# Memory of x given early to half of the left forms, in a hybrid RWKV-7 and short-convolution block

## The chip, the core and the metric

The kernel runs on one core of a Trainium2 chip. Five engines matter here: TensorE (PE in the profile) multiplies 128x128 weights with up to 512 columns; VectorE (DVE), ScalarE (ACT) and GpSimd (POOL) work on rows of 128 partitions; SyncE (SP) issues most transfers. Each engine works through its own queue in order, and the engines wait for one another by semaphores. The metric is the time of one execution in microseconds (us).

## The reference: what is computed

The input x has 512 rows of 2048 numbers; 16 learned meta rows are put ahead, which makes 528. Cut to what matters here:

```python
hn = _rmsnorm(h_res, norm_in_g[l])
P = hn @ w_in[l]                      # 528 x 2048 times 2048 x 8320
Pr, Pc = P[..., :RW_COLS], P[..., RW_COLS:]
...                                   # group A: RWKV-7 recurrence on r, k, v, decay, a; gate g_r
y_a = (yn + bonus) * jax.nn.silu(g_r)
Bg, Cg, hc, g_c = (four parts of Pc, 1024 columns each)
y_b = Bg * _causal_depthwise_conv(Cg * hc, conv_w[l]) * jax.nn.silu(g_c)
mix = jnp.concatenate([y_a, y_b], axis=-1)
h_res = h_res + mix @ w_out[l]        # 512 x 2048 times 2048 x 2048
out = _rmsnorm(h_res, norm_f_g)
```

All of it is float32. The change concerns the end of the first product (`w_in`) and the beginning of the last one (`w_out`).

## The kernel before, in words

**Split numbers.** TensorE multiplies in a shorter format (float32r). To keep float32's accuracy, each operand is split into a high part, which ACT makes by a cast, and a low part, which DVE makes by subtracting the high part from the original. A product is three matmuls: high by high, high by low, low by high. For x the parts are `xh` and `xl`, two tiles of 16 column blocks (k) by 528 rows, filled by `split_x` at the start. For a half piece of weights they are `wh` and `wl` (`split_w`, L124 and L125) in the projection, `oh` and `ol` (`split_unit`, L1171 and L1172) in the output projection. The buffers of these pieces rotate: six of each.

**The projection.** `main` runs one tile of 128 output columns at a time, in 65 tiles. A tile goes through k in four quarters (`k4`), and `steps` issues the matmuls of one quarter (L312). After a tile, `use` evacuates PSUM with the row scale (`scaled`, L331) and does the tile's own arithmetic. The last four tiles are C, h, B and gc of convolution block 7; for gc the arithmetic is L331 on DVE, tanh on ACT (L358), and on DVE L359 and L422, which writes block 15 of the mix. L359 reads scratch tiles of the pool `tp`.

**The mix and the left forms.** `mix` is four tiles of four column blocks by 512 rows: tiles 0 and 1 are the recurrence's blocks 0 to 7, tiles 2 and 3 the convolution's blocks 8 to 15. `split_mix` finishes a block and splits it (L1061, L1062; tile `m`). The output projection is done by a Strassen-like scheme with seven products, M1, P5, M7, M3, Q6, P4 and M2. Four of them take sums of quarters of the mix on the left: `sums(q)` (L1070 to L1075) forms these sums in place, for half q of the column blocks, by four DVE operations on 128x1024 numbers; `split_form(f, q)` (L1117, L1118; tile `S`) splits one of the four forms S1, S3, S4, S5 of half q by one ACT cast and one DVE subtraction of 128x1024. Each form occupies two tiles of 128x1024 numbers in the pool `pw`.

**Order of the output projection.** `units` is a list of (half, product, group): first the four groups of M1, then for each group P5, M7, M3 and Q6, then P4 and M2; and the same for the second half. A unit is 12 matmuls of 512 columns with one group of rows of w_out, in two pieces. Groups 0 and 1 use the forms of half q = 0, groups 2 and 3 those of q = 1. In the profile's names the product's letter is shown without its digit, so that M1, M7, M3 and M2 are all `M`; M1 reads `m` on the left, the others of the first four groups `S`. `at(u, fn, ...)` puts work ahead of unit u: in the kernel before, `split_form(f, 0)` is called at units 0 to 3, `sums(1)` at unit 3 and `split_form(f, 1)` at units 6 to 9. The right-hand pieces for M1's groups 0 to 2 are loaded and split during the projection (the stream's last three entries). Group 3's rows go into a tile of `pw` (`begin_chain`, L1148), a pool that takes the place of the projection's pools when these are closed (`ph1.close()`, L1100).

**What sets the order.** PE's order is written by hand: the generator `flow` yields matmul by matmul, and `fill`, `step` and the loops interleave other work. For DVE, ACT, POOL and SP the planner of the tile framework sets the order, by the position in the program, by `tc.high_priority` (the weight splits have it) and by when it reckons an operand to be ready; `tc.issue_after(ins)` puts an instruction behind `ins` on the same engine. A tile that takes over memory waits for the last reader of the tile that had it (`reuse_waits="tile"`).

Of the kernel before, what the change touches and what calls it, by code (L numbers as in the profile page):

```python
# [9 lines left out]
F32 = mybir.dt.float32  # L10
# [8 lines left out]
P = 128  # L19
DM = 2048  # L20
KT = DM // P
# [55 lines left out]
def hymba_kernel(ctx: ExitStack, tc: tile.TileContext, xt, xtok, front, w_in, w_out, pv, lup, cst, msk, gf, out):  # L77
# [62 lines left out]
    cq = ph2.enter_context(tc.tile_pool(name="cq", bufs=1, side="right", reuse_waits="tile"))  # L140
    ph1 = ExitStack()
    xp = ph1.enter_context(tc.tile_pool(name="xp", bufs=1))
    xh = xp.tile([P, KT, L], F32R, name="xh")
    xl = xp.tile([P, KT, L], F32R, name="xl")
    rs = xp.tile([P, L], F32, name="rs")
    la = xp.tile([P, 2, L], F32R, name="la")
    ones = xp.tile([P, P + 2], F32R, name="ones")
# [8 lines left out]
    scr_x = [dp.tile([SCR], F32, tag=f"sx{b}", name=f"sx{b}", bufs=1) for b in range(2)]  # L156

    tp = ph1.enter_context(tc.tile_pool(name="tp", bufs=1))

    def tr(name, dt=F32):  # L160
        return cq.tile([P, LP], dt, tag="tr", name=name, bufs=5)
# [28 lines left out]

    def split_x(kt, cols=slice(0, L)):
        gain = ng[:, kt : kt + 1]
        nc.scalar.activation(xh[:, kt, cols], raw[kt][:, cols], AF.Copy, scale=gain)
        return nc.vector.scalar_tensor_tensor(
            out=xl[:, kt, cols], in0=raw[kt][:, cols], scalar=gain, in1=xh[:, kt, cols].bitcast(F32),
            op0=ALU.mult, op1=ALU.subtract,
        ).ins

# [104 lines left out]
    def steps(ps, ranges, k4, q, ks=range(4), rs_=range(2)):  # L303
        hi, lo = quarters[q]
        for r, (a, b) in enumerate(ranges):
            if r not in rs_:
                continue
            for k in ks:
                kt = 4 * k4 + k
                w = slice(k * P, (k + 1) * P)  # L310
                for n, (ww, xx) in enumerate(((hi, xh), (hi, xl), (lo, xh))):
                    nc.tensor.matmul(  # L312
                        ps[r], ww[:, w], xx[:, kt, a:b], start=(kt == 0 and n == 0), stop=(kt == KT - 1 and n == 2)
                    )
                    yield (b - a) * 0.43

# [747 lines left out]

    forms = {"S3": (0, T1), "S5": (0, T0), "S1": (2, T1), "S4": (2, T0)}

    def quarter(k, tk, q):
        return mix[2 * k + q][:, :, tk]

    def sums(q):  # L1070
        a11, a21, a12, a22 = quarter(0, T0, q), quarter(0, T1, q), quarter(1, T0, q), quarter(1, T1, q)
        nc.vector.tensor_tensor(out=a22, in0=a22, in1=a21, op=ALU.subtract)
# [40 lines left out]
    def split_form(f, q):  # L1113
        k, tk = forms[f]
        x = mix[k + q][:, :, tk]
        hi, lo = sform[f, q]
        nc.scalar.copy(hi, x)  # L1117
        nc.vector.tensor_tensor(out=lo, in0=x, in1=hi.bitcast(F32), op=ALU.subtract)  # L1118


    LEFT = {"M1": 0, "M2": T0, "M7": "S3", "Q6": "S5", "P5": "S1", "P4": T1, "M3": "S4"}
# [41 lines left out]
    def split_unit(unit, t, home=None):  # L1163
        for q in range(2):
            rq = t()[:, q * 512 : (q + 1) * 512]
            if home is None:
                hi = wp.tile([P, 512], F32R, tag="hi", name=f"oh{U[unit]}{q}", bufs=6)
                lo = wp.tile([P, 512], F32R, tag="lo", name=f"ol{U[unit]}{q}", bufs=6)
            else:
                hi, lo = home[q]  # L1170
            nc.scalar.copy(hi, rq)  # L1171
            nc.vector.tensor_tensor(out=lo, in0=rq, in1=hi.bitcast(F32), op=ALU.subtract)  # L1172
            right[unit, q] = (hi, lo)

    def here(t, n):
# [148 lines left out]
    for u, unit in enumerate(units):  # L1324
# [150 lines left out]
```

## Time and profile before

| what | value |
|---|---|
| median of 3 timed runs | 1026.73 us (1024.77 to 1630.5) |
| profiled execution | 1021.34 us |
| its span (first to last instruction) | 1019.6 us |
| PE busy | 1005.0 us, 99% of the span |
| DVE busy | 684.2 us, 67% |
| ACT busy | 394.6 us, 39% |
| POOL busy | 274.7 us, 27% |
| last projection tile (gc of block 7) on PE | 840.27 us, for 11.14 us |
| output projection on PE, first unit | 851.24 us |

The profile is that of one execution; all times within it count from the start of the span. The profiled execution's own time is that of the span and what lies around it, and the timed runs are others. PE is busy almost throughout, so that what counts is where it is not: the waits of PE, what ends them, and the chain of work that ended last. "Busy" for PE is modelled, because matmuls overlap; the start of one matmul against the start of the next shows lost time more truly than the idle column.

### The profile page before, as it was taken

Reading aid. Unit: us, or ns where it says so; the run is one execution under the profiler, and the core shown is the slowest. Engines: PE = TensorE matmul, PEld = TensorE weight load, DVE = VectorE, ACT = ScalarE, POOL = GpSimd, SP = SyncE. Lnnn points to the kernel's source line nnn. Section 1 sums busy time; section 2 is a strip of 40 time slices with the busy share of each in tenths; the row PEclk is TensorE's granted clock in tenths of the full one; section 3 lists DMA queues with packets and bytes.
Section 4 is the critical chain, followed back from the end, with each engine's and each line's share of the span. In section 5 each row is a group of like instructions: output and inputs, shape, how many; then the busy total and the mean of one; then the engine's idle time right before and its main releaser. Section 6 shows DMA issues by size and latency. Waiting matters only on the chain.

```text
span 1019.6 us, 23707 instructions
## 1 busy us (share of the span) xinstructions
PE 1005.0 (99%) x9723; PEld 917.8 (90%) x9723; DVE 684.2 (67%) x1235; ACT 394.6 (39%) x727; POOL 274.7 (27%) x294
## 2 busy tenths in 40 slices
PE   9999999999999999999999999999999999999996
PEld 7899998999998999998999998889889897787885
DVE  7877765568655569654669653244555697999786
ACT  7544322534322434322424322222222335445453
POOL 0132323323232323232323222223332332005001
PEclk9999999999999999999999999999999999999999
DMA  9436386364864263853273846877672687695644
GB/s 315 146 106 167 84 219 189 98 166 103 214 171 138 84 168 102 216 150 117 83 178 100 209 139 180 299 225 235 194 229 86 197 272 189 168 320 138 173 124 165
DMA packets 184892, 174.82 MB, mean 171 GB/s; under 512 B 121552, under 2 KB 142672, under 8 KB 184400
## 3 DMA queue, kind: packets, MB, share of 16 engines
q1 hardware_dynamic: 182192, 164.40, 54.1%
q0 software_dynamic: 2304, 8.39, 4.8%
q8 instruction: 76, 1.25, 0.5%
q10 hardware_dynamic: 288, 0.52, 0.1%
q14 instruction: 32, 0.26, 0.1%
HBM read 136.92 MB, written 36.35 MB: 170 GB/s over the span
## 4 chain that ended last, share of the span: by engine, by line
PE 90%; DVE 4%; DMA 3%; ACT 1%; issue 1%; SPq 0%; DVEq 0%; POOL 0%; ACTq 0%
PE ps_v L312 9%; PE ps_h L312 9%; PE ps_g L312 9%; PE ps_B L312 9%; PE ps_gc L312 9%; PE ps_k L312 9%; PE ps_C L312 8%; PE ps_r L312 8%; PE M L1199 4%; PE P L1199 3%; PE Q L1199 2%; PE g L638 2%; DVE ol L1172 1%; PE zs L963 1%; PE zy L967 1%
## 5 line engine op out<-in xcount | busy, mean ns | idle before, releaser
L125 POOL TENSOR_TENSOR wl<-wr,wh 128x512 fp32r<-128x512 f32 x121 | 170.3, 1408 | 371.6 <-ACT wh L124 349.4
L124 ACT CAST wh<-wr 128x512 fp32r<-128x512 f32 x254 | 154.0, 618 | 299.1 <-PE ps_k L312 52.3
L125 DVE TENSOR_TENSOR wl<-wr,wh 128x512 fp32r<-128x512 f32 x133 | 98.9, 752 | 107.3 <-ACT wh L124 106.2
L312 PE MATMUL ps_v<-xh,wh 128*128 128x264 f32 x256 | 73.1, 286 | 0.0
L312 PE MATMUL ps_k<-xh,wh 128*128 128x264 f32 x256 | 73.0, 285 | 0.0
L312 PE MATMUL ps_h<-xh,wh 128*128 128x258 f32 (+1 forms) x256 | 72.9, 285 | 0.1
L312 PE MATMUL ps_k<-xh,wl 128*128 128x264 f32 x256 | 73.0, 285 | 0.0
L312 PE MATMUL ps_r<-xh,wl 128*128 128x258 f32 (+1 forms) x256 | 72.1, 282 | 0.7 <-DVE wl L125 0.7
L312 PE MATMUL ps_v<-xh,wl 128*128 128x264 f32 x256 | 72.7, 284 | 0.0
L312 PE MATMUL ps_v<-xl,wh 128*128 128x264 f32 x256 | 72.7, 284 | 0.0
L312 PE MATMUL ps_k<-xl,wh 128*128 128x264 f32 x256 | 72.6, 284 | 0.0
L312 PE MATMUL ps_C<-xh,wh 128*128 128x258 f32 (+1 forms) x256 | 72.6, 284 | 0.0
L312 PE MATMUL ps_g<-xl,wh 128*128 128x258 f32 (+1 forms) x256 | 72.4, 283 | 0.0
L312 PE MATMUL ps_h<-xh,wl 128*128 128x258 f32 (+1 forms) x256 | 72.2, 282 | 0.0
L312 PE MATMUL ps_r<-xh,wh 128*128 128x258 f32 (+1 forms) x256 | 72.1, 282 | 0.0
L312 PE MATMUL ps_C<-xl,wh 128*128 128x258 f32 (+1 forms) x256 | 72.0, 281 | 0.0
L312 PE MATMUL ps_r<-xl,wh 128*128 128x258 f32 (+1 forms) x256 | 72.0, 281 | 0.0
L312 PE MATMUL ps_g<-xh,wh 128*128 128x258 f32 (+1 forms) x256 | 72.0, 281 | 0.0
L312 PE MATMUL ps_h<-xl,wh 128*128 128x258 f32 (+1 forms) x256 | 71.9, 281 | 0.0
L312 PE MATMUL ps_g<-xh,wl 128*128 128x258 f32 (+1 forms) x256 | 71.9, 281 | 0.0
L312 PE MATMUL ps_C<-xh,wl 128*128 128x258 f32 (+1 forms) x256 | 71.9, 281 | 0.0
L312 PE MATMUL ps_B<-xl,wh 128*128 128x512 f32 x128 | 51.0, 399 | 0.0
(344 smaller groups left out, 3001.2 us busy)
## 6 DMA issues: line engine op xcount, KB each, us to landing
wr<-in_w_in_dram SPq DMA_DIRECT2D x127, 512.0 KB
ct<-opd SPq DMA_DIRECT2D x64, 288.0 KB
wo<-in_w_out_dram SPq DMA_DIRECT2D x24, 512.0 KB
x<-in_w_out_dram POOLq DMA_DIRECT2D x16, 512.0 KB, 5.6
opd<-ar SPq DMA_DIRECT2D x8, 576.0 KB
opd<-gt SPq DMA_DIRECT2D x16, 288.0 KB
opd<-bt SPq DMA_DIRECT2D x64, 64.0 KB
x<-in_w_out_dram SPq DMA_DIRECT2D x8, 512.0 KB
```

The source lines that it names most:

```text
L124: nc.scalar.copy(hi, rq)
L125: low[q] = eng.tensor_tensor(out=lo, in0=rq, in1=hi.bitcast(F32), op=ALU.subtract).ins
L312: nc.tensor.matmul(ps[r], ww[:, w], xx[:, kt, a:b], start=(kt == 0 and n == 0), stop=(kt == KT - 1 and n == 2))
L638: nc.tensor.matmul(z[h][:, c - c0], bk[hs, c, h : h + 2, :].rearrange("p a s -> p (a s)"), ar[hs, c].rearrange("p a s -> p (a s)"), start= ...
L963: nc.tensor.matmul(d[hs, j], w, x[hs], start=(a == 0), stop=(a == b - 1))
L967: nc.tensor.matmul(d[ho, j], t[hs, o : o + CH], x[hs], start=(a == 0), stop=(a == b - 1))
L1172: nc.vector.tensor_tensor(out=lo, in0=rq, in1=hi.bitcast(F32), op=ALU.subtract)
L1199: nc.tensor.matmul(bank[s], left(prod, jj, m, s), w, start=(jj == 0 and n == 0), stop=(jj == 7 and n == 2))
```

## The change

The two tiles `xh` and `xl` become eight, one for each quarter of k. The first two quarters of both lie in a pool `xq` of their own, the other two in `xp`. When the last projection tile has issued its first two quarters (`k4 == 2`), `xq` is closed, and a pool `ps` with the forms of half q = 0 is opened; those four forms are split there at once, ahead in the program of the rest of that tile and its evacuation. `sums(1)` is done in two parts: column blocks 0 to 2 of the half (of 128x768 numbers) before the last projection tile's `step` loop, block 3 (128x256) at unit 3, as before. The forms of q = 1 are called at units 6 to 9 as before, but by `late_form`, which puts them behind the last split that the program issued by unit 1. The home tiles of the second half's M2 pieces, which reuse the forms' memory, come from `ps` too.

```diff
-    xh = xp.tile([P, KT, L], F32R, name="xh")
-    xl = xp.tile([P, KT, L], F32R, name="xl")
...
+    ph0 = ExitStack()
+    xq = ph0.enter_context(tc.tile_pool(name="xq", bufs=1))
+    xh, xl = ([(xq if k4 < 2 else xp).tile([P, 4, L], F32R, name=f"{n}{k4}") for k4 in range(4)] for n in ("xh", "xl"))
...
-        nc.scalar.activation(xh[:, kt, cols], raw[kt][:, cols], AF.Copy, scale=gain)
+        hi, lo = (x[kt // 4][:, kt % 4, cols] for x in (xh, xl))
+        nc.scalar.activation(hi, raw[kt][:, cols], AF.Copy, scale=gain)
...
-                        ps[r], ww[:, w], xx[:, kt, a:b], start=(kt == 0 and n == 0), stop=(kt == KT - 1 and n == 2)
+                        ps[r], ww[:, w], xx[k4][:, k, a:b], start=(kt == 0 and n == 0), stop=(kt == KT - 1 and n == 2)
...
+            if k4 == 2 and j == len(plan) - 1:
+                state["half"] = True
...
-    def sums(q):
-        a11, a21, a12, a22 = quarter(0, T0, q), quarter(0, T1, q), quarter(1, T0, q), quarter(1, T1, q)
+    def sums(q, rows=slice(0, 4)):
+        a11, a21, a12, a22 = (mix[2 * k + q][:, rows, tk] for k in range(2) for tk in (T0, T1))
...
+    sform = {}
+
+    def new_forms(pool, q):
+        for f in forms:
+            sform[f, q] = [pool.tile([P, 4, HT], F32R, tag=f"{f}{q}{a}", name=f"{f}{q}{a}") for a in range(2)]
...
     for j in range(NPAIR + 4, KT):
+        if j == KT - 1:
+            sums(1, slice(0, 3))
+            while "half" not in state:
+                step()
+            ph0.close()
+            ps = ctx.enter_context(tc.tile_pool(name="ps", bufs=1, side="right", reuse_waits="tile"))
+            new_forms(ps, 0)
+            for f in ("S1", "S3", "S4", "S5"):
+                split_form(f, 0)
         while ("gc", j - NPAIR) not in ready:
             step()
...
-    sform = {
-        (f, q): [pw.tile([P, 4, HT], F32R, tag=f"{f}{q}{a}", name=f"{f}{q}{a}") for a in range(2)]
-        for q in range(2) for f in forms
-    }
+    new_forms(pw, 1)
...
+    def late_form(f):
+        with tc.issue_after(state["first"]):
+            split_form(f, 1)
...
-            nc.vector.tensor_tensor(out=lo, in0=rq, in1=hi.bitcast(F32), op=ALU.subtract)
+            state["last"] = nc.vector.tensor_tensor(out=lo, in0=rq, in1=hi.bitcast(F32), op=ALU.subtract).ins
...
-            pw.tile([P, 4, HT], F32R, tag=f"{f}0{a}", name=f"home{g}{a}").rearrange("p a b -> p (a b)") for a in range(2)
+            ps.tile([P, 4, HT], F32R, tag=f"{f}0{a}", name=f"home{g}{a}").rearrange("p a b -> p (a b)") for a in range(2)
...
     for n, f in enumerate(("S1", "S3", "S4", "S5")):
-        at(n, split_form, f, 0)
         if n == 2:
-            at(n + 1, sums, 1)
-        at(6 + n, split_form, f, 1)
+            at(n + 1, sums, 1, slice(3, 4))
+        at(6 + n, late_form, f)
...
+        if u == 1:
+            state["first"] = state["last"]
```

More of the change, by code (lines that the diff above doesn't have):

```diff
@@ L192, in split_x @@
         gain = ng[:, kt : kt + 1]
-        nc.scalar.activation(xh[:, kt, cols], raw[kt][:, cols], AF.Copy, scale=gain)
+        hi, lo = (x[kt // 4][:, kt % 4, cols] for x in (xh, xl))
+        nc.scalar.activation(hi, raw[kt][:, cols], AF.Copy, scale=gain)
         return nc.vector.scalar_tensor_tensor(
-            out=xl[:, kt, cols], in0=raw[kt][:, cols], scalar=gain, in1=xh[:, kt, cols].bitcast(F32),
+            out=lo, in0=raw[kt][:, cols], scalar=gain, in1=hi.bitcast(F32),
             op0=ALU.mult, op1=ALU.subtract,
@@ L1065, in hymba_kernel @@
     forms = {"S3": (0, T1), "S5": (0, T0), "S1": (2, T1), "S4": (2, T0)}
-    def quarter(k, tk, q):
-        return mix[2 * k + q][:, :, tk]
-    def sums(q):
-        a11, a21, a12, a22 = quarter(0, T0, q), quarter(0, T1, q), quarter(1, T0, q), quarter(1, T1, q)
+    def sums(q, rows=slice(0, 4)):
+        a11, a21, a12, a22 = (mix[2 * k + q][:, rows, tk] for k in range(2) for tk in (T0, T1))
         nc.vector.tensor_tensor(out=a22, in0=a22, in1=a21, op=ALU.subtract)
@@ L1091, in hymba_kernel, with split_form @@
     chain.update({g: new_chain(0, g) for g in range(3)})
-    for j in range(NPAIR + 4, KT):
+    sform = {}
+    def new_forms(pool, q):
+        for f in forms:
+            sform[f, q] = [pool.tile([P, 4, HT], F32R, tag=f"{f}{q}{a}", name=f"{f}{q}{a}") for a in range(2)]
+    def split_form(f, q):
+        k, tk = forms[f]
+        x = mix[k + q][:, :, tk]
+        hi, lo = sform[f, q]
+        nc.scalar.copy(hi, x)
+        nc.vector.tensor_tensor(out=lo, in0=x, in1=hi.bitcast(F32), op=ALU.subtract)
+    for j in range(NPAIR + 4, KT):
+        if j == KT - 1:
[7 more added lines that the diff above has]
+                split_form(f, 0)
         while ("gc", j - NPAIR) not in ready:
@@ L1106, in hymba_kernel @@
     fv = pw.tile([P, 4, 3], F32, name="fv")
-    sform = {
-        (f, q): [pw.tile([P, 4, HT], F32R, tag=f"{f}{q}{a}", name=f"{f}{q}{a}") for a in range(2)]
-        for q in range(2) for f in forms
-    }
+    new_forms(pw, 1)
     xa = [pw.tile([P, 1024], F32, name=f"xa{t}") for t in range(4)]
[L1113 to L1118, printed above, removed]
+    def late_form(f):
+        with tc.issue_after(state["first"]):
+            split_form(f, 1)
     LEFT = {"M1": 0, "M2": T0, "M7": "S3", "Q6": "S5", "P5": "S1", "P4": T1, "M3": "S4"}
```

## The prediction

> **What bounds the kernel now.** I first read how busy each engine is and which engines make up the chain that ended last.
>
> ```profile
> span 1019.6 us, 23707 instructions
> PE 1005.0 (99%) x9723; PEld 917.8 (90%) x9723; DVE 684.2 (67%) x1235; ACT 394.6 (39%) x727; POOL 274.7 (27%) x294
> PE 90%; DVE 4%; DMA 3%; ACT 1%; issue 1%; SPq 0%; DVEq 0%; POOL 0%; ACTq 0%
> ```
>
> PE is idle for 1019.6 - 1005.0 = 14.6 us in all, and the chain runs over PE for nine tenths of the span. The change neither adds nor removes a matmul. So whatever it gives must come out of those 14.6 us, which are 1.4% of the span. A gain of 2% is not there to be had. Next come PE's waits by releaser, and in the timeline of PE the places in the reach of the change.
>
> ```profile
> PE M L1199 <- DVE ol L1172: 1.0, 3, 0.5
> PE Q L1199 <- DVE ol L1172: 0.6, 1, 0.6
> ...
> 851.24 0.40 PE L1199 MATMUL M<-wh,m 128*128 128x512 f32 x1
> ...
> 860.40 0.50 PE L1199 MATMUL M<-ol,m 128*128 128x512 f32 x1 [0.22 <-DVE ol L1172]
> ...
> 863.07 0.40 PE L1199 MATMUL P<-oh,S 128*128 128x512 f32 x1
> ...
> 870.30 0.50 PE L1199 MATMUL M<-ol,S 128*128 128x512 f32 x1 [0.53 <-DVE ol L1172]
> ...
> 873.23 0.50 PE L1199 MATMUL Q<-ol,S 128*128 128x512 f32 x1 [0.56 <-DVE ol L1172]
> ...
> 875.90 0.39 PE L1199 MATMUL P<-oh,S 128*128 128x512 f32 x1
> ...
> 939.12 0.50 PE L1199 MATMUL M<-ol,m 128*128 128x512 f32 x1 [0.27 <-DVE ol L1172]
> ...
> 890.29 5.60 PE M L1199 x24
> ```
>
> All four waits of the output projection are for `ol`, the low part of a piece of w_out, which DVE writes at L1172. The modelled idle times add up to 1.6 us, but the starts tell more. The last row is an undisturbed run of 24 matmuls in 5.60 us, or 2.80 us for a unit of 12. From 851.24 the four M1 units should end at 862.44, but the first P5 unit starts at 863.07: **0.63 us lost in the fourth M1 unit**. From there four units should end at 874.27, but the next starts at 875.90: **1.63 us lost in M3 and Q6 of group 0**. The wait at 939.12 is worth 0.27 us.
>
> What makes DVE late there is shown by the chain in order of time, and by the busy time of each engine in three stretches (PE, PEld, DVE, ACT, POOL in that order).
>
> ```profile
> 851.44 0.70 DVE gc L331
> ...
> 852.83 0.70 DVE gc L359
> ...
> 853.55 5.36 DMA x<-in_w_out_dram
> ...
> 859.00 0.63 ACT oh L1171
> ...
> 859.66 0.56 DVE ol L1172
> ...
> 872.57 0.61 DVE ol L1172
> ...
> 838.50:851.40 12.90, 12.90 (x57) 10.49 (x56) 7.33 (x11) 4.00 (x8) 6.08 (x4) 1.00 0.82 201
> 851.40:862.90 11.50, 11.28 (x48) 8.65 (x48) 10.11 (x13) 8.48 (x13) 1.76 (x2) 1.00 0.70 191
> 862.90:873.30 10.40, 9.30 (x40) 6.87 (x38) 10.40 (x14) 8.09 (x13) 0.00 (x0) 1.00 0.51 129
> ```
>
> Two different things end the waits. The fourth M1 unit waits for a **transfer**: its rows of w_out can only be requested once L359 has read the projection's scratch tile that lies under them (852.83 and 0.70 us, so 853.53), and the 5.36 us of transfer, ACT's 0.63 and DVE's 0.56 bring the first `ol` at 860.2. It has no slack. M3 and Q6 of group 0 wait for **DVE's queue**: in 862.9 to 873.3 DVE is busy for all 10.40 us. The granted clock is 1.00 in all three.
>
> **The change part by part.** The rows for the costs are these: the last projection tile and the first late unit in the chain, PE's wait at the start, the groups of DVE and ACT, and DVE's idle times before the end of the projection.
>
> ```profile
> 840.27 11.14 PE ps_gc L312 x48
> 887.49 2.80 PE P L1199 x12
> ...
> PE ps_lora L312 <- DVE xl L194: 1.0, 2, 0.7
> ...
> L1118 DVE TENSOR_TENSOR S<-mix,S 128x1024 fp32r<-128x1024 f32 x8 | 9.7, 1220 | 0.0
> L1072 DVE TENSOR_TENSOR mix<-mix,mix 128x1024 f32<-128x1024 f32 x1 | 1.2, 1224 | 0.0
> L1062 DVE TENSOR_TENSOR m<-mix,m 128x512 fp32r<-128x512 f32 x3 | 2.0, 683 | 0.7 <-ACT m L1061 0.7
> L1117 ACT CAST S<-mix x8: 1046/1050/1057, 854.9 to 869.7; 128x1024 fp32r<-128x1024 f32 x8
> ...
> 838.53 1.61 DVE L1062 TENSOR_TENSOR m<-mix,m 128x256 fp32r<-128x256 f32 x3
> ...
> 843.31 1.38 DVE L1161 TENSOR_TENSOR wo<-wo,wo 128x1024 f32<-128x1024 f32 x1 [0.85 <-DMA wo<-in_w_out_dram]
> ...
> 846.35 0.69 DVE L125 TENSOR_TENSOR wl<-x,wh 128x512 fp32r<-128x512 f32 x1 [1.05 <-ACT wh L124]
> 849.08 0.69 DVE L125 TENSOR_TENSOR wl<-x,wh 128x512 fp32r<-128x512 f32 x1 [2.03 <-ACT wh L124]
> 851.44 0.69 DVE L331 TENSOR_TENSOR gc<-ps_gc,rs 128x512 f32<-128x512 f32 x1 [1.67 <-PE ps_gc L312]
> 852.04 0.68 DVE L125 TENSOR_TENSOR wl<-x,wh 128x512 fp32r<-128x512 f32 x1
> ...
> 830.58 0.42 DVE L1062 TENSOR_TENSOR m<-mix,m 128x256 fp32r<-128x256 f32 x1
> ```
>
> *Four splits of the first forms move up.* Four DVE subtractions of 1.22 us (4.88 us) and four ACT casts of 1.05 us (4.20 us) leave the stretch after 851.4. They can start when the last projection tile has done its first two quarters of k. That tile runs from 840.27 to 851.41, so its half is near 845.8; a cast of 1.05 us later, DVE can begin at about 846.9.
>
> *The second sums are cut.* Today there are four operations of 128x1024, 4 x 1.22 = 4.88 us, all after 855.7. Three quarters of each (768 elements) fall between 0.68 us (512) and 1.22 us (1024); I take the middle, 0.95. They wait for the splits that read the same rows, the last of which end at 838.53 + 1.61 = 840.14. The last quarter (256 elements) costs 0.42 us. So 3.80 us go before 851.4 and 1.68 us stay: 0.60 us more work altogether, but 4.88 - 1.68 = 3.20 us less after 851.4.
>
> *Relief.* After 851.4 DVE loses 4.88 + 3.20 = **8.08 us** of the 20.51 us that it worked between 851.4 and 873.3. The four splits of the second forms may come in earlier in its place (4 x 1.22 = 4.88 us), which would leave 3.20 us. Both are more than the 1.63 us by which M3 and Q6 were late, and the buffers for M3's pieces are those of the fourth M1 unit, free at 863.07 where M3, two units of 2.80 us later, needs them at 868.7. I take the whole **-1.63 us**. The wait at 939.12 is 65 us away behind other transfers: between 0 and -0.27, I take 0.
>
> *The price.* From 840.14 to 851.44 DVE gets 3.80 + 4.88 = 8.68 us more. Its idle times there are 0.85 + 1.05 + 2.03 + 1.67 = 5.60 us. So some 3 us don't fit. The add of 1.38 us at 843.31 belongs to a later unit and may give way, but of the four form splits only three of 1.22 us fit into the 3.70 us idle after 847; the fourth meets the evacuation of the projection's last tile at 851.44. That evacuation starts the chain L331, ACT's tanh, L359, transfer, fourth M1 unit, which has no slack: each microsecond of it is a microsecond of PE. The bounds: 0 if the order on DVE puts the evacuation first, and at most 846.9 + 4 x 1.22 + 2 x 0.69 = 853.2 for its start, with 0.6 more if the sums push the first split back, so 2.4 us. I take one split, **+1.2 us**. On ACT the four casts fit beside the weight casts (the gaps of 1.05, 2.03 and 1.67 us in which DVE waits for a weight cast or for PE are gaps of ACT too, and I expect the casts done by about 851.5); the casts of the second forms, which the change does not hold back on ACT, could stand in front of the fourth M1 unit's cast at 859.00: 0 to 1.05 us. I take 0, since today's casts do not.
>
> *The other edits.* Eight tiles for x: the same casts, subtractions and matmuls on the same columns; 0, with the start's two waits for the low part of x (1.0 us) as the bound either way. The new wait of the form casts on PE's first half stands in front of ACT's remaining weight casts and so of DVE's `wl`; the last of those is written at 852.04 to 852.72, and the third M1 unit needs it near 857.5, so up to 4.8 us of delay cost nothing. SP's queue gets no transfer more; its request for the fourth M1 unit moves with the evacuation, and the two requests of xa behind it with that. POOL issues the same accumulating transfers. The late forms' wait on the fourth M1 unit's split only keeps them out of DVE's way; the first unit that needs them is P5 of group 2, which starts at 887.49.
>
> *Sum*: -1.63 + 1.2 = -0.4 us, and with the bounds from -1.63 - 0.27 = -1.9 to -1.63 + 2.4 + 1.05 = +1.8 us. The start's bound of 1.0 us widens this to -2.9 and +2.8.
>
> One more thing happens where the added work goes. POOL's product and DVE's subtraction overlap here:
>
> ```profile
> 833.78 1.30 POOL L402 TENSOR_TENSOR u<-u,hh 128x514 f32<-128x514 f32 x1 [0.96 <-DVE hh L331]
> ...
> 833.84 1.52 DVE L1062 TENSOR_TENSOR m<-mix,m 128x256 fp32r<-128x256 f32 x1
> ...
> 839.48 2.43 POOL L125 TENSOR_TENSOR wl<-wr,wh 128x512 fp32r<-128x512 f32 x1 [4.41 <-ACT wh L124]
> 841.87 1.74 POOL L415 TENSOR_TENSOR cv<-cv,b 128x512 f32<-128x512 f32 x1
> ```
>
> The DVE row of 256 elements takes 1.52 us instead of 0.42 while POOL works, and ends with it; POOL's row at 839.48 takes 2.43 us where its neighbour took 1.30. One waits for the other. The first sums fall upon POOL's rows at 839.48 and 841.87. Two such waits cost DVE up to 2 x 1.1 = 2.2 us. POOL's last product there is needed only at L422, about 853.6.
>
> The Trainium skill, "SBUF — State Buffer", section "Who interferes with whom", says that a VectorE instruction with two SBUF inputs and a GpSimd instruction that reads SBUF exclude each other for a whole instruction. The trace agrees with it in the 1.52 us row. By that rule the moved sums are dearer than in my sum, and the forecast would turn into the rival below called the lock.
>
> **The rivals.**
> *The evacuation falls back (the other side).* All four splits and part of the sums stand ahead of L331 on DVE. For it speaks that they are issued by the program before the evacuation and that 8.68 us meet 5.60 us of idle time. Against it speaks that weight splits still found their place in this queue when DVE was full. It decides from a delay of 1.63 us, where it has eaten the gain; at 2.4 us it gives +0.8, with ACT's cast +1.8.
> *The lock.* POOL's reads stretch the sums by up to 2.2 us, and this delay reaches L331 too: -1.63 + 1.2 + 2.2 = +1.8 us. Against it: the sums come 7 us or more before L331, and the 1.9 us of idle time before 846.4 can swallow most.
> *All gain, no price.* The evacuation stands first and the wait at 939 goes as well: -1.9 us.
> *The change does not do what it says.* The splits get their memory but are still placed behind the evacuation, since the order on DVE is the planner's: then only the sums move, and the relief of 3.20 us still covers the 1.63: -1.6, or, where the second forms fill it, 0.
> *A disturbance elsewhere.* The planner orders ACT, DVE and POOL of the whole program afresh, and a badly placed wait in front of the weight splits could starve PE again and again. Nothing in the trace asks for it; 2% would be 20.5 us, that is over seven units of 2.80 us lost whole.
>
> **How the numbers follow.** The profiled execution took 1021.34 us with a span of 1019.6, so 1.7 us lie around the span; the median of the timed runs is 1026.73, 5.4 us above it, and the lowest is 1024.77. Thus the spread between executions is larger than anything in my sum. I carry the sum over to the median: 1026.73 - 0.4 = 1026.3 us. In the profiled execution's terms it is 1021.34 - 0.4 = 1020.9.
> Chances: the forecast, with between -1.2 and +0.4 us, 0.45; all gain or the sums alone 0.20; evacuation late 0.20; the lock 0.10; a disturbance elsewhere 0.05, of which 0.03 is over 2%. The range begins at the profiled execution's level with the largest gain, 1021.34 - 1.9 = 1019.4, which I round up to 1020, since the median stood higher; it ends at 1026.73 + 1.8 + the 2 us between the two lower times = 1030.5. About 2% is what a measurement of this kernel can tell from no change, 1006 to 1047. Faster by over 2% needs more idle time than PE has: 0.01. Slower by over 2%: 0.03. The rest, 0.96, is within 2%.
>
> **What would show it.** If the relief is right, PE's rows for M3 and Q6 of group 0 show no wait for `ol`, the first P5 unit of group 1 starts 11.20 us after that of group 0, and DVE has idle time between 862.9 and 873.3. If the price is right, L331's evacuation starts about 1.2 us after the projection's last matmul instead of at once, and the fourth M1 unit's transfer and its wait move by the same. If the move was made, the L1117 casts start about 846, before the evacuation. I am wrong if L331 starts more than 2.4 us late, if M3 or Q6 still waits for DVE, or if PE waits in the projection where it did not before.

## The result, and the profile after

The changed kernel takes 1029.26 us (median of 8 runs, 1027.49 to 1031.48), the kernel before 1024.56 us beside it. The ratio is 1.0051, with a 95% interval from 1.0034 to 1.0069: some 5 us slower, by less than the 2% named in the prediction, but clearly not the 0.4 us faster that I forecast. The ratio is formed from the fast runs alone, without one run of the kernel before that took 1630.5 us, and so isn't the quotient of the two medians. The profiled execution took 1027.49 us with a span of 1025.4 us, where before it was 1021.34 and 1019.6 us.

First the page of the changed kernel, how busy the engines are:

```profile
span 1025.4 us, 23710 instructions
...
PE 1008.6 (98%) x9723; PEld 921.3 (90%) x9723; DVE 687.3 (67%) x1239; ACT 396.4 (39%) x727; POOL 274.5 (27%) x294
```

Of the 5.8 us more of span, PE is *busy* for 3.6 us, although it does the same 9723 matmuls. So the loss isn't waiting alone: some matmuls have become slower. Next, PE's waits by releaser in the changed kernel (us in total, times, longest), the longest of them:

```profile
PE M L1217 <- ACT oh L1189: 3.9, 1, 3.9
```

The waits of M3 and Q6 for `ol` are gone. In their place stands one wait of 3.9 us for ACT's `oh`. The timeline of PE in the changed kernel shows where:

```profile
851.99 0.40 PE L315 MATMUL ps_gc<-xh,wl 128*128 128x512 f32 x1
852.22 0.39 PE L1217 MATMUL M<-wh,m 128*128 128x512 f32 x1
...
864.67 0.79 PE L1217 MATMUL M<-oh,m 128*128 128x512 f32 x1 [3.89 <-ACT oh L1189]
865.39 0.79 PE L1217 MATMUL M<-ol,m 128*128 128x512 f32 x1
865.99 1.05 PE L1217 MATMUL M<-oh,m 128*128 128x512 f32 x2
...
870.25 0.63 PE L1217 MATMUL P<-oh,S 128*128 128x512 f32 x1
...
873.34 0.39 PE L1217 MATMUL M<-oh,S 128*128 128x512 f32 x1
...
881.74 0.39 PE L1217 MATMUL P<-oh,S 128*128 128x512 f32 x1
...
944.76 0.50 PE L1217 MATMUL M<-ol,m 128*128 128x512 f32 x1 [0.28 <-DVE ol L1190]
```

The fourth M1 unit should begin 3 x 2.80 = 8.40 us after 852.22, at 860.62. It begins at 864.67, **4.05 us late**, and takes until 870.25, which is 5.58 us instead of 2.80: **2.78 us more**. Not all of that is slow matmuls. From 865.99 on, ten steps from start to start take 4.26 us, so twelve at this pace would take 5.11; the other 0.47 us lie in the first two steps (0.72 and 0.60 us), at the first `ol`, which came late in the kernel before too. From there the four units of group 0 take 881.74 - 870.25 = 11.49 us, where the kernel before took 12.83 and an undisturbed run 11.20. The wait at 944.76 is the old one at 939.12.

The chain in order of time in the changed kernel (start, us, what) leads back from that wait:

```profile
856.85 0.61 DVE gc L336
...
857.49 0.64 ACT th_c L363
...
858.15 0.70 DVE gc L364
...
858.87 5.02 DMA x<-in_w_out_dram
...
864.00 0.63 ACT oh L1189
...
864.67 5.79 PE M L1217 x12
```

It is the chain of before, L331 (now L336), tanh, L359 (now L364), transfer, fourth M1 unit. In the kernel before, the evacuation began 0.20 us after the first output matmul (851.44 against 851.24); now it begins at 856.77 (below), 4.55 us after it. So it is **4.35 us late**. The transfer is 0.34 us shorter; what is left, about 4.0 us, is the delay of the unit.

Busy time in stretches of the changed kernel (PE, PEld, DVE, ACT, POOL, granted clock, DMA share, GB/s), the three stages of the prediction, and shorter stretches around the fourth M1 unit:

```profile
838.50:851.40 12.90, 12.90 (x57) 10.43 (x56) 12.80 (x16) 8.24 (x13) 4.51 (x3) 1.00 0.50 164
851.40:862.90 11.50, 9.38 (x41) 7.22 (x39) 9.83 (x14) 3.41 (x6) 1.75 (x2) 1.00 0.80 164
862.90:873.30 10.40, 8.63 (x24) 6.57 (x25) 7.78 (x11) 8.32 (x14) 0.89 (x1) 0.67 0.72 214
...
864.00:864.60 0.60, 0.00 (x0) 0.00 (x0) 0.00 (x0) 0.60 (x2) 0.00 (x0) 0.53 0.99 403
...
865.00:866.00 1.00, 1.00 (x3) 0.51 (x3) 1.00 (x3) 1.00 (x3) 0.00 (x0) 0.50 0.74 303
...
870.00:871.00 1.00, 1.00 (x4) 0.77 (x3) 1.00 (x2) 0.63 (x2) 0.00 (x0) 0.57 0.99 197
871.00:872.00 1.00, 1.00 (x6) 0.81 (x5) 1.00 (x3) 0.60 (x2) 0.00 (x0) 1.00 0.90 295
```

Before the end of the projection DVE was busy for 7.33 of 12.90 us; now for 12.80. It has no idle time left there. And near the end of the long wait the granted clock falls to 0.50, where it stays until about 870.86: three or four matmuls per microsecond instead of six. (A mean of 0.53 over 864.00 to 864.60 puts the fall at 864.04, one of 0.57 over 870.00 to 871.00 the rise at 870.86, so the low clock lasts 6.8 us.) That is the second half of the loss. The timeline of DVE in the changed kernel shows what filled it up, and that of POOL two overlaps:

```profile
841.06 1.94 DVE L1074 TENSOR_TENSOR mix<-mix,mix 128x768 f32<-128x768 f32 x1
843.03 0.96 DVE L1075 TENSOR_TENSOR mix<-mix 128x768 f32<-128x768 f32 x1
...
845.51 0.95 DVE L1077 SCALAR_TENSOR_TENSOR mix<-mix,mix 128x768 f32<-128x768 f32 x1
...
847.58 2.33 DVE L1179 TENSOR_TENSOR wo<-wo,wo 128x1024 f32<-128x1024 f32 x1
...
851.03 3.48 DVE L1105 TENSOR_TENSOR S<-mix,S 128x1024 fp32r<-128x1024 f32 x3
...
855.04 1.21 DVE L1105 TENSOR_TENSOR S<-mix,S 128x1024 fp32r<-128x1024 f32 x1
...
856.77 0.68 DVE L336 TENSOR_TENSOR gc<-ps_gc,rs 128x512 f32<-128x512 f32 x1
```

```profile
840.37 1.82 POOL L125 TENSOR_TENSOR wl<-wr,wh 128x512 fp32r<-128x512 f32 x1 [4.41 <-ACT wh L124]
847.14 1.68 POOL L420 TENSOR_TENSOR cv<-cv,b 128x512 f32<-128x512 f32 x1 [4.95 <-DVE b L336]
```

All four sums and all four form splits stand ahead of the evacuation at 856.77. The sums take 1.94 + 0.96 + 0.96 + 0.95 = 4.81 us (the third, at 844.03, is like the second), the splits 3.48 + 1.21 = 4.69, and the add of 1.38 us before now takes 2.33. That is 4.81 + 4.69 + 0.95 = 10.45 us more against the 5.60 us of idle time counted before: 4.85, where the delay is 4.35. The difference is made of small things: rows that follow one another overlap by up to 0.09 us, one weight split that stood behind the evacuation before (852.04) now stands ahead of it (856.17), and another is no longer stretched (1.19 us at 841.27 before). Counted from start to start, DVE has 9.94 us more to do there, and 9.94 - 5.60 = 4.34. The two long rows, 1.94 and 2.33, are those that lie beside a POOL row that reads SBUF. The Trainium skill, "SBUF — State Buffer", section "Who interferes with whom", says that such a pair excludes each other; the trace agrees. The second overlap is the sums' own doing: they put off the evacuation of tile B of block 7 on DVE from 840.67 to 846.38, and POOL's product at 847.14, which waits for it, now falls upon the add.

### The profile page after: what moved, and what is told of

Read it like the earlier page. It is cut to its first block, busy times and chain, and to the rows that moved or that the text cites. A ratio compares the mean times of both kernels' runs of the same rounds, so it can differ in the third digit from the quotient of the medians.

```text
span 1025.4 us, 23710 instructions
## 1 busy us (share of the span) xinstructions
PE 1008.6 (98%) x9723; PEld 921.3 (90%) x9723; DVE 687.3 (67%) x1239; ACT 396.4 (39%) x727; POOL 274.5 (27%) x294
## 3 DMA queue, kind: packets, MB, share of 16 engines
q0 software_dynamic: 2304, 8.39, 4.9%
## 4 chain that ended last, share of the span: by engine, by line
PE 84%; DVE 8%; issue 3%; DMA 2%; ACT 1%; SPq 0%; POOL 0%; DVEq 0%; ACTq 0%; POOLq 0%
PE ps_v L315 9%; PE ps_g L315 9%; PE ps_k L315 9%; PE ps_r L315 8%; PE ps_h L315 8%; PE ps_C L315 8%; PE ps_B L315 8%; PE ps_gc L315 8%; PE M L1217 4%; PE g L643 2%; PE P L1217 2%; DVE ol L1190 2%; DMA wo<-in_w_out_dram 1%; PE Q L1217 1%; PE zs L968 1%
```

## The experiments

The table has, for each kernel's profile, the first output matmul ("M1"), the time from there to the first P5 unit of group 0 and from that to the one of group 1 (undisturbed 11.20 each, four units of 2.80), and the "tail", the span's end less M1. The tail leaves out what happened in the projection, where M1 differs by up to 4 us between executions. What is left of it behind the P5 unit of group 1 takes 143.4 to 144.6 us in these profiles, though PE has the same work there, so the tails tell differences of about 1 us and no finer ones.

| kernel | M1 | to P5, group 0 | to P5, group 1 | tail |
|---|---|---|---|---|
| before | 851.24 | 11.83 | 12.83 | 168.4 |
| after | 852.22 | 18.03 | 11.49 | 173.2 |
| e1_tiles | 853.14 | 11.32 | 12.82 | 168.2 |
| e2_early_rows | 855.36 | 12.10 | 12.25 | 167.9 |
| e3_forms_only | 854.95 | 15.21 | 11.20 | 170.0 |
| e4_evac_8_times | 852.61 | 19.06 | 11.80 | 174.3 |
| e5_sums_only | 854.82 | 11.72 | 11.21 | 166.4 |
| e6_rows_first | 852.00 | 11.65 | 11.20 | 167.4 |
| e7_splits_behind | 854.06 | 11.37 | 11.20 | 166.4 |
| e8_x_moved | 853.41 | 11.85 | 12.82 | 169.1 |
| e9_evac_3_times | 854.40 | 13.25 | 12.83 | 170.5 |

**My theory after these profiles**: the late evacuation starts a chain without slack; its wait lowers the granted clock; together that is the loss. **Rivals**: that the eight tiles or the planner's new order elsewhere cost the time; that the forms alone, or the sums alone, do it.

### A late evacuation alone

The kernel before, with the evacuation of the last projection tile issued eight times over; nothing of the change is in it.

```diff
-            scaled(REAL, ps, g, META)
+            for _ in range(8 if i == NPAIR - 1 else 1):
+                scaled(REAL, ps, g, META)
```

> The kernel before, with the evacuation of the last projection tile done eight times over into the same tile (seven of them superfluous, 0.60 us each, 4.2 us in all), and nothing of the change. Theory A: the fourth M1 unit waits 0.2 + 4.2 = 4.4 us and its matmuls then run at the half clock as in the changed kernel (12 in 5.8 us instead of 2.8): +6 to +8 us against before, less what DVE catches up in the wait (up to 1.6): +5 to +7. Rival (the loss in the changed kernel comes from elsewhere): +4.2 or less.

Measured: 1028.46 us, ratio 1.0051 (1.0038 to 1.0065), the same loss as the whole change. The timeline of PE in this kernel, at the fourth M1 unit, and one of its microseconds in the windows:

```profile
865.32 0.50 PE L1200 MATMUL M<-oh,m 128*128 128x512 f32 x1 [4.13 <-ACT oh L1172]
...
866.81 0.80 PE L1200 MATMUL M<-ol,m 128*128 128x512 f32 x1 [1.00 <-DVE ol L1173]
```

```profile
869.00:870.00 1.00, 1.00 (x4) 0.72 (x4) 1.00 (x3) 1.00 (x3) 0.00 (x0) 0.50 0.59 66
```

A wait like that of the changed kernel, the same clock of 0.50 behind it, and the same time. So a delay of this size at this place is enough for the loss, without any part of the change. (The tail is even 1.1 us longer than the changed kernel's, and x lies where it did.) By itself this doesn't show that nothing else costs time in the changed kernel; the next ones bear on that. And M3 and Q6 of group 0 lose their waits here too (11.80 instead of 12.83, a part of it at the low clock), though nothing was moved: while PE waits, DVE catches up.

The same edit with three times instead of eight, for the point at which the clock falls:

> The kernel before with the last tile's evacuation done three times over (two of them superfluous, 1.2 us). The fourth M1 unit then waits about 0.2 + 1.2 = 1.4 us, between the 0.56 us at which the clock did not fall and the 1.98 us at which it did. Theory C1 (any wait of more than a microsecond makes the clock fall): granted clock 0.5 for about 3 us after the wait, and the unit takes 5.5 us or more. Theory C2 (it takes about 2 us, or depends on where the wait lies): clock 1.0, the unit takes 2.8 + 1.6 us.

Measured, in one execution each, which can't tell much: 1026.84 us beside 1022.14. Its timeline of PE and a microsecond of its windows:

```profile
864.13 0.51 PE L1200 MATMUL M<-oh,m 128*128 128x512 f32 x1 [1.16 <-ACT oh L1172]
...
864.98 0.50 PE L1200 MATMUL M<-ol,m 128*128 128x512 f32 x1 [0.34 <-DVE ol L1173]
```

```profile
866.00:867.00 1.00, 1.00 (x6) 0.80 (x5) 1.00 (x3) 1.00 (x2) 0.88 (x1) 1.00 0.00 0
```

With 1.16 and 0.34 us of waiting the clock stays at 1.00 through the unit. Here the wait cost only itself.

### The forms alone, the sums alone

The changed kernel with the second sums whole again at unit 3:

```diff
-            sums(1, slice(0, 3))
...
-            at(n + 1, sums, 1, slice(3, 4))
+            at(n + 1, sums, 1)
```

> The changed kernel with the second sums whole at unit 3 again, so that only the form splits are early. DVE then gets 4.9 us instead of some 10 us more before the evacuation, against 5.6 us of idle time, with three weight splits between. Theory A: the evacuation starts 1 to 2 us late instead of 4.5; the fourth M1 unit waits 1.5 to 2.5 us, which is too short for the clock to fall; so 3 to 5 us faster than the changed kernel, and within 1 us of before. Rival (the form splits alone make the delay): the wait stays near 3.9 us and the time near the changed kernel's.

Measured: 1025.49 us, ratio 1.0024 (1.0014 to 1.0035). DVE's timeline in this kernel, PE's row of the fourth M1 unit, and short stretches around it:

```profile
847.88 1.23 DVE L1178 TENSOR_TENSOR wo<-wo,wo 128x1024 f32<-128x1024 f32 x1 [1.81 <-DMA wo<-in_w_out_dram]
...
850.99 3.50 DVE L1105 TENSOR_TENSOR S<-mix,S 128x1024 fp32r<-128x1024 f32 x3 [0.26 <-ACT S L1104]
...
856.74 0.68 DVE L336 TENSOR_TENSOR gc<-ps_gc,rs 128x512 f32<-128x512 f32 x1
```

```profile
865.48 0.68 PE L1216 MATMUL M<-oh,m 128*128 128x512 f32 x1 [1.98 <-ACT oh L1188]
```

```profile
865.48:866.00 0.52, 0.52 (x1) 0.19 (x1) 0.52 (x1) 0.52 (x2) 0.00 (x0) 0.65 0.57 229
866.00:867.00 1.00, 0.95 (x3) 0.69 (x3) 1.00 (x3) 1.00 (x3) 0.00 (x0) 0.50 0.19 78
...
869.00:870.00 1.00, 1.00 (x6) 0.82 (x5) 0.99 (x2) 1.00 (x2) 0.00 (x0) 0.97 0.95 78
```

The evacuation begins 856.74 - 854.95 = 1.79 us after the first output matmul, 1.59 late. That is close to the 1.2 of the prediction: with the forms alone, three of the four splits do fit, and the fourth and a weight split (at 856.14) stand ahead of the evacuation. Nonetheless the unit loses 15.21 - 11.20 = 4.01 us: 2.13 of late start and 1.88 within the unit, 0.47 of it again in the first two steps and 1.41 by slow matmuls. For already this wait of 1.98 us is followed by a clock of 0.50, from 865.64 (0.65 in the first stretch) to 869.06 (0.97 in the last), which is 3.4 us. I had expected it to stay. The other 2.8 us of the whole change's delay belong to the sums and the stretched add, which takes 1.23 us here, with no POOL arithmetic beside it. M3 and Q6 of group 0 have no wait left (11.20), but as they come behind a wait of PE, that doesn't yet show that the forms bring the relief.

Now the kernel before with the sums in two parts and nothing else:

```diff
+        if j == KT - 1:
+            sums(1, slice(0, 3))
...
-            at(n + 1, sums, 1)
+            at(n + 1, sums, 1, slice(3, 4))
```

> The kernel before with only the second sums in two parts; x in its two tiles, the forms late as before. DVE gets about 4.5 us more against 5.6 us of idle time before the last evacuation. Theory A (what hurt was an overfull DVE in front of the evacuation): the evacuation starts at once or less than 0.7 us late, no fall of the clock, and of the 1.63 us in M3 and Q6 of group 0 most goes: from the first M1 unit to the end -1 to -1.6 us against before, and no cost from the layout. Rival (the sums, which meet POOL's reads, are what delayed the evacuation): it starts 1.5 us late or more and the gain is gone.

Measured: 1021.70 us beside 1023.15, ratio 0.9985 (0.9971 to 1.0000). DVE's evacuation row and PE's only row with a wait in the fourth M1 unit of this kernel:

```profile
855.01 0.69 DVE L331 TENSOR_TENSOR gc<-ps_gc,rs 128x512 f32<-128x512 f32 x1 [0.21 <-PE ps_gc L312]
```

```profile
863.88 0.50 PE L1198 MATMUL M<-ol,m 128*128 128x512 f32 x1 [0.23 <-DVE ol L1171]
```

The sums fit into the idle time: the evacuation still waits for PE, with 0.21 us to spare, and the four units of group 0 take 11.21 us. The whole relief of 1.63 us comes with this small part of the change alone, and with no long wait of PE ahead of it. The early forms weren't needed for it.

### Mending the changed kernel

Two ways to keep the early forms. First, the rows of the fourth M1 unit go into a tile of the early pool, so that their transfer no longer waits for L364:

```diff
+            chain[3] = ps.tile([P, 1024], F32, tag="X3", name="x03")
+            behind(chain[3], w_out[0, 3])
...
-                    at(-1, begin_chain, 0, g)
```

> The changed kernel with the rows of the fourth M1 unit taken into the early pool too (over the second quarter of x) and requested there, so that they no longer wait for the last projection tile's evacuation. Theory A: the evacuation still starts 4 us or more late, but nothing on PE hangs on it; no PE wait of more than 0.5 us in the M1 units, no fall of the granted clock at 860 to 870, and M3 and Q6 of group 0 without a wait: 6 to 7 us faster than the changed kernel, 1 to 2 us faster than before. Rival (the loss comes from DVE being overfull as such, or from the layout of x): no more than 2 us faster than the changed kernel.

Measured: 1025.13 us, ratio 1.0017 (1.0006 to 1.0027). The evacuation is as late as in the changed kernel (859.90 against M1 at 855.36), but no long wait follows and the clock stays at 1.00. In its place stand two waits for DVE, in the timeline of PE of this kernel:

```profile
864.80 0.50 PE L1219 MATMUL M<-ol,m 128*128 128x512 f32 x1 [0.31 <-DVE ol L1192]
...
869.33 0.50 PE L1219 MATMUL P<-ol,S 128*128 128x512 f32 x1 [0.77 <-DVE ol L1192]
```

The tail falls by 5.2 us from that of the changed kernel, which confirms that the loss hung on this transfer. But DVE's backlog of 4.35 us doesn't vanish; it meets PE a little later, and the two groups of units take 12.10 and 12.25 us instead of 11.20. I had expected 1 to 2 us less than before. The kernel stays 0.2% slower, although its tail is 0.5 us below that of before: the rest of the loss lies outside the tail.

Second, the four splits are held behind the gate (L364) on DVE, with the rest of the change as it is:

```diff
+            with tc.issue_after(state["gate"]):
+                for f in ("S1", "S3", "S4", "S5"):
+                    split_form(f, 0)
```

> The changed kernel with the four early form splits held behind the last tile's gate step on DVE (the casts on ACT stay early). Theory A: the evacuation starts within 0.7 us of the last projection matmul, the fourth M1 unit waits less than 0.7 us, the clock does not fall; from the first M1 unit to the end -0.5 to -1.6 us against before and some 6 us less than the changed kernel; with the layout's cost of about 1.4 us in the projection it comes out within 1 us of before. Rival: the wait stays over 1.5 us, because the sums and not the splits delay DVE.

Measured: 1023.97 us, ratio 1.0000 (0.9985 to 1.0015). DVE's evacuation in this kernel:

```profile
854.26 0.69 DVE L336 TENSOR_TENSOR gc<-ps_gc,rs 128x512 f32<-128x512 f32 x1 [0.72 <-PE ps_gc L315]
```

It starts at once, both groups of units run almost undisturbed (11.37 and 11.20), and the tail is, with that of the sums alone, the shortest in the table, 1.9 us below before. Yet the time is that of before. Something outside the tail takes those 1.9 us, as in the run above, and that is the next question.

### The place of x

The kernel before with x in eight tiles (the diff of the change around `xq`, `split_x` and `steps`), and nothing moved early:

> The kernel before with x in eight tiles and nothing else moved: the forms stay in the late pool, the second sums stay whole at unit 3. Theory A (the delayed evacuation makes the loss): no loss here; the evacuation stands where it stood before. In this layout the fourth M1 unit's rows lie over the second low quarter of x instead of over the projection's scratch tile, so their transfer can go at about half of the last projection tile, and the 0.6 us lost in that unit go too: 0 to -0.7 us against before. Theory B (the layout of x slows the projection's matmuls; the changed kernel's 96-matmul tiles took 11.39 us where before's took 11.36): every tile at 11.39, +1 to +2 us in all, whatever happens at the end.

Measured: 1023.85 us beside 1023.44, ratio 1.0009 (0.9998 to 1.0019). The tail is 0.2 us shorter, as the fourth M1 unit's rows now lie over another tile and come in time; M3 and Q6 wait as before. So it should be faster, and isn't: by the medians and the tails some 0.6 us went in the projection, though the interval allows for none. The chains in order of time tell it more sharply, by the C tile, 96 matmuls, of which four come 151 us apart. The first and the fourth of them, in the kernel before and then in the changed one:

```profile
124.99 11.36 PE ps_C L312 x96
...
577.62 11.36 PE ps_C L312 x96
```

```profile
124.83 11.39 PE ps_C L315 x96
...
578.24 11.39 PE ps_C L315 x96
```

From the first to the fourth it is 452.63 us before and 453.41 after: 0.78 us. It is 453.39 in the kernel with the eight tiles alone, 453.37 to 453.39 in the other three so far that have them, and 452.62 to 452.68 in the three kernels above that leave x in two tiles. Over the projection's 847 us or so (from the first matmuls to 851) this is some 1.4 us, an estimate from the 452.6.

Is it the number of tiles or where they lie? In the kernel before, x left in two tiles but allocated behind the small ones, 9536 bytes further:

```diff
-    xh = xp.tile([P, KT, L], F32R, name="xh")
-    xl = xp.tile([P, KT, L], F32R, name="xl")
     rs = xp.tile([P, L], F32, name="rs")
...
+    xh = xp.tile([P, KT, L], F32R, name="xh")
+    xl = xp.tile([P, KT, L], F32R, name="xl")
```

> The kernel before with x's two tiles as they are, but behind the pool's small tiles, so at other addresses (9.5 KB higher); nothing else. Theory B1 (the place in memory slows the matmuls): 96 matmuls of a C tile in 11.39 us as with eight tiles, +0.8 us between the first C tile and the fourth, +1.4 us in all. Theory B2 (the number of tiles does): 11.36 us and no difference from before.

Measured: 1025.46 us beside 1023.15, ratio 1.0013 (1.0000 to 1.0025). Its chain in order of time:

```profile
124.97 11.47 PE ps_C L312 x96
...
578.94 11.47 PE ps_C L312 x96
```

Here it is 453.97 from the first to the fourth, and the same 96 matmuls take 1% longer. By the stretch it would be 1.34 x 847 / 452.6 = 2.5 us for the whole projection, an estimate at the upper end of the interval. Neither the number of tiles nor the program's order was touched: it is the **place** of x in memory. (The pool's small tiles moved as well, but these matmuls don't read them.) Two more shifts were run once each, 64 bytes (a small tile ahead of x) and 2304 bytes (the tile `smask` ahead of it):

> The kernel before with x's two tiles 64 bytes higher. If the matmuls' slowness follows the place of x in fine steps, the C tiles take more or less than 11.36 us (11.47 with 9536 bytes); if it follows only coarse steps (kilobytes), 11.36 us. About 1 us at most in all, which one look cannot tell in the time; the reading is the length of the tiles in the chain.

> The kernel before with x's two tiles 2304 bytes higher (the mask tile ahead of them). Same reading as with 64 bytes: C tiles at 11.36 us if the place does not matter at this distance, 11.39 to 11.47 us if it does.

At 64 bytes the tile takes 11.47 us and the stretch 454.10 (1023.82 us in all); at 2304 bytes 11.36 and 452.64 (1024.78 us), beside 1022.14 for the kernel before. The times of one execution don't settle it, the lengths in the chain do. 64 and 9536 are odd multiples of 64, 2304 and the place before even ones. From this I tried to mend the held-back splits with 64 bytes of padding:

```diff
+    pad0 = xp.tile([P, 16], F32, name="pad0")
...
+    pad1 = tp.tile([P, 16], F32, name="pad1")
```

> The changed kernel with its four early form splits behind the last tile's gate step, as in the run before, and every tile of x 64 bytes higher (two small tiles put in). If the layout's cost in the changed kernel follows 64-byte steps as it did for one tile, the C tiles go from 11.39 to 11.36 us and the whole is 1 to 1.5 us faster than the run with the splits behind, that is 1 to 1.5 us faster than before (ratio 0.9985). If the eight tiles cost something of themselves, 11.39 us stays and the ratio is 1.000.

Measured: 1022.79 us beside 1022.18, ratio 1.0000 (0.9991 to 1.0008). The C tiles take 11.38 to 11.41 us, not 11.36, and from the first to the fourth it is 453.05, between the 452.63 of before and the 453.38 without the padding. The shift mended it at most in part. It also wasn't quite the one described: in the program as built, the two pads raise the last two quarters of x by 64 bytes and the first two, which lie behind both pads, by 128. With them all eight tiles are even multiples of 64 bytes from the place before, and yet not at 11.36.

Without the pads the first two quarters are an even multiple away (56704 bytes) and the last two an odd one (9536). The starts of the matmuls in a C tile don't follow that either: 24 of them take 2.84 us in each quarter of k before and 2.87 with x moved by 9536 bytes, and in the changed kernel 2.86 in the first quarter and 2.84 in the second and third. So the rule of odd and even multiples fails with eight tiles. That the place matters is shown, for x in its two tiles; by which rule, and whether with eight tiles their number adds something, stays open.

### The sums, and the rows first

The sums in two parts, and the fourth M1 unit's tile allocated first in `pw`, so that it lies over x and not over the scratch that L359 reads:

```diff
+    chain[3] = pw.tile([P, 1024], F32, tag="X3", name="x03")
     ssq = pw.tile([P, 4, 5], F32, name="ssq")
...
-        if half or g == 3:
+        if half:
```

> As the run with the sums alone, and the tile for the rows of the fourth M1 unit stands first in the late pool, over the high part of x instead of over the projection's scratch: its transfer waits for the last projection matmul only, about 2 us earlier than before. Theory A: the 0.63 us in the fourth M1 unit go too: -1.5 to -2.2 us against before from the first M1 unit to the end. Rival (the unit waits for DVE's order, not for the transfer): no difference from the run with the sums alone.

Measured: 1021.53 us beside 1023.15, ratio 0.9982 (0.9967 to 0.9997). One wait is left in the fourth M1 unit, in the timeline of PE of this kernel:

```profile
860.98 0.49 PE L1199 MATMUL M<-ol,m 128*128 128x512 f32 x1 [0.17 <-DVE ol L1172]
```

This beats both kernels, by 0.2% and 0.7% (0.9982 / 1.0051 = 0.993; the two weren't measured side by side). Over the sums alone its gain can't be told: the two intervals nearly coincide. The rows come earlier, but DVE puts form splits ahead of their `ol`, and the unit still takes 11.65 - 8.40 = 3.25 us. Of the 0.63 us that it lost before, only some 0.2 are gone, and by the tail this kernel is 1.0 us below before, where I had expected 1.5 to 2.2.

## Why the prediction was wrong

*Relief, -1.63 us: right in its size.* M3 and Q6 of group 0 wait no more. 12.83 became 11.49, and the missing 0.29 is the clock, still low in the first of the four units (870.25 to 873.34, 3.09 instead of 2.80). In this kernel the number is partly luck, since the long wait alone removes most of it (11.80 with the evacuation eight times over and nothing moved). That the mechanism holds without such a wait is shown by the sums alone (11.21) and by the splits held back (11.20). And I credited the wrong part with it: the cut sums alone give it, the moved splits nothing more.

*The price, +1.2 us and at most 2.4: the step that failed.* Its mechanism, the rival in which the evacuation falls back, is what happened, at the place and by the chain that I named. Its size was wrong: 4.35 us late. I priced the splits against the idle time after 847 as if the 3.80 us of sums had been swallowed before it. For the splits alone that holds (1.59 late with the forms only, where I took 1.2). Together 10.45 us met 5.60. I had written that some 3 us don't fit, and then didn't carry them into the price: I let the first split begin at 846.9 and the evacuation at 853.8 at the latest, but the first split began at 851.03 and the evacuation at 856.77, where M1 lies 0.98 us later than before. By the sign that I had named, L331 more than 2.4 us late, the price is refuted. The hope that the add "may give way" failed as well: the add stood ahead of the splits and grew from 1.38 to 2.33.

*The lock: partly.* Two rows of DVE were stretched beside POOL, by 1.94 - 0.95 = 0.99 and 2.33 - 1.38 = 0.95, 1.9 us in all, near the 2.2 that I gave it. What I set against it, that the sums come 7 us before the evacuation and idle time can swallow the delay, was wrong, since no idle time was left to swallow it. I held it for a rival of its own, where it adds to the others. A small misreading too: the stretched rows don't end with POOL's row but 0.3 to 1.1 us after it.

*A missing step: the clock.* I read that the granted clock was 1.00 in all three stretches and didn't ask what a longer wait would do to it. At the low clock the unit lost 5.11 - 2.80 = 2.31 us and the next one 0.29, so the wait of 3.89 us cost 2.60 us on top of itself.

*Eight tiles of x, 0 (bound 1.0): wrong.* They cost some 1.4 us in the projection, by the estimate from the C tiles; the timed run of the eight tiles alone gives -0.2 to 1.9 us. That a place in memory can do this is shown for x in two tiles; for the eight tiles it is likely, not shown.

*Right at nothing*: a disturbance elsewhere (PE's longest waits in the projection are 0.9, 0.7 and 0.7 us, as before), the wait at 939 (0.27 before, 0.28 now), the weight casts behind the form casts (M1's first three units run through) and ACT's casts of the forms, which in ACT's timeline of the changed kernel stand well before the evacuation:

```profile
847.18 2.95 ACT L1104 CAST S<-mix 128x1024 fp32r<-128x1024 f32 x3
```

The account, in the profiles: late start of the unit +4.05; its wait for the first `ol` 0.47 instead of 0.63, -0.16; clock +2.60; relief -1.63; together +4.86, where the tails differ by 4.82 (so close by chance, as tails tell no more than about 1 us). With the estimate of 1.4 for x it is 6.2, against 5.8 by the two spans and 4.7 by the medians (3.5 to 7.1 by the interval). 1029.26 lies within my range, but the range reached so far up because of the spread between executions, not because I had the mechanism's size.

## What to carry to other kernels

When work is moved into idle time of an engine that works its queue in order, set *all* of the added work, stretched by its neighbours, against *all* of the idle time, and look at what stands behind it in the queue: here an evacuation at the head of a chain with no slack. Take the smallest part of an edit that removes the wait; the cut sums gave the whole gain, and the costly part added only the loss. A wait on the engine that bounds the kernel may cost more than its length, and a tile that merely lies elsewhere may cost something too, so profile each of them by itself.

## What I had not expected of the hardware

- **The clock falls after short waits.** A wait of 1.98 us was followed by a granted clock of 0.50 for 3.4 us. With waits of 3.89 and 4.13 us the low clock lasted 6.8 us each time, in the first case from 0.6 us before the wait's end on. With 1.16 and 0.34 us there was none. The Trainium skill, "TensorE: Matmul & The Clock Gate", section "What's actually happening", has the clock fall after at least one idle window of about 3.4 us. That window is longer than the 1.98 us that were enough here, and the measurement decides; that the low clock lasted 3.4 us or twice that agrees with windows of this length. At which wait between 1.2 and 2.0 us it begins, and whether that is the same each time, no run here shows.
- **The place of the moving operand changes the pace of matmuls.** 96 matmuls of the C tile take 11.36 us with x where it was and 2304 bytes further, 11.47 at 64 and 9536 bytes, and 11.38 to 11.41 with x in eight tiles. The four places of the whole x fit a rule of odd and even multiples of 64 bytes, but the eight tiles break it, so the rule is open.
